# One five-block raw tile for each weight pair in place of two tiles, the sums written over blocks already split, three such tiles

## The chip, the core and the metric

The kernel runs on one core of a Trainium2 chip. The core has a matrix engine (TensorE, PE in the rows), VectorE (DVE), ScalarE (ACT), GpSimd (POOL) and SyncE (SP, which here only starts DMA transfers), each with an instruction queue of its own that it works off in order. The metric is the device time of one execution in microseconds; the median of several runs is compared.

## The reference

The reference computes one layer of a decoder trunk on 512 tokens of width 1024, in float32:

```
h = rmsnorm(x, norm_g)
proj = h @ w_in               # 14 groups of columns, about 14,400 in all
yA = mLSTM(aq, ak, av, ai, af) * norm * sigmoid(ao) * silu(az)   # 4 heads of 256
yB = forgetting_attention(bq, bk, bv, bf) * silu(bz)             # 8 heads of 128
yC = multiscale_pool(cu) * silu(cz)                              # 4 groups of 256
merged = sum over n of sigmoid(gates[n]) * (y[n] @ w_branch[n])
out = rmsnorm(x + merged @ w_out, final_g)
```

The kernel is free in how it multiplies, as long as the float32 result is met.

## The kernel before

**Split products.** Each float32 matrix is split into a high part (`hi`, a cast to a rounded format on ScalarE, `hi_of`, line 288) and a low part (`lo`, the difference, on VectorE, `lo_of`, line 291). A product is then three matmuls (`mm3`, lines 300 to 302): hi by hi, hi by lo, lo by hi.

**Units and pairs.** The weights are read in the order that `plan()` gives. A unit ("U") is one weight tile of 128x1024 that is loaded, split and multiplied as it is. A pair ("P") is two column groups of 128 that are multiplied together by a seven-product scheme of the Strassen kind: the 1024x256 weight block is seen as four blocks of 128x512 (Q = 512 columns in memory), and the products need sums of them. There are 42 pairs. For each, the kernel before keeps two raw tiles: R, 128x1536, with the three blocks b2_1, b1_0, b1_1 as loaded, and T, 128x2048, whose first two blocks are loaded as b2_1 and b1_0. GpSimd then starts a DMA that adds the block b2_0 onto both (line 377), and VectorE adds two further blocks (T2 = T1 + R0 and T3 = T2 + R2, lines 392 and 396). The splits are called parts: j = 0 takes the last two blocks of R, j = 1 the first of R, j = 2 takes T1 and T2, j = 3 takes T0 and T3. PE uses them in the order 0, 0, 2, 2, 3, 1, 3, twelve matmuls each, into the PSUM tiles `x`, `yz` and `y4` (function `pair`).

**Where raw data lies.** R and T have two buffers each. A unit takes a buffer of either kind, whichever is free first. The halves of a split go to one of four slots, and small tiles lie in a pool `w` of 11 buffers.

**What sets the order.** The instruction order is written by a planner at build time (`Flow`): it keeps a clock for each engine, gives each operation an estimated cost (`v_cost`, `a_cost`) and each transfer an estimated landing time (for the DMA that adds, 4.2 us after it is started), and records an operation on its engine when its estimated start has come. Nothing is reordered on the chip: an operation that waits holds up all that is recorded behind it on its engine. A transfer is started on SP when its buffer is free, in recorded order as well. The weight item numbers in tile names count the plan: `T16` is the second tile of item 16 (the pair ak_2, ak_3), `lo15_3` the low half of part 3 of item 15 (aq_2, aq_3), `raw43` the raw tile of unit 43 (a pool weight, "pw").

**Stages.** First head (units, to about 78 us), three mLSTM heads, pooling, four attention stages (pairs of bq and bk, units of bv, pairs of bz), the last gates (to about 689 us), then the branch products `wb` and the output product, which use units alone.

Of the kernel before, what the change touches and what calls it, by code (L numbers as in the profile page):

```python
# [7 lines left out]
F32 = mybir.dt.float32  # L8
# [5 lines left out]
P = 128  # L14
S = 512
D = 1024
KT = D // P
NT = S // P
AH = 4
# [10 lines left out]
SWITCH = 1.3  # L30
NEAR = 4
PLAIN = 2

C_NG = 0
C_MNG = 8
# [53 lines left out]
def v_cost(n):  # L89
    return 0.15 + 1.05e-3 * n  # L90
# [16 lines left out]
class Flow:  # L107
# [39 lines left out]
    def settle(self, c):  # L147

        while c.alive:
            kind = c.req[0]  # L150
            if kind == "get":
                t = self.grab(*c.req[1:])
                if t is None:
                    return False
                self.resume(c, t)
            elif kind == "any":
                names = [n for n in c.req[1] if self.free[n]]
                if not names:
                    return False
                n = min(names, key=lambda n: self.free[n][0])  # L160
                self.resume(c, (n, self.grab(n)))
# [88 lines left out]
def trunk(tc, x, xt_in, w, wpair, cols, fg, out):  # L250
    nc = tc.nc
    with contextlib.ExitStack() as ctx:
# [14 lines left out]
                index.append(np_)  # L267
                np_ += 1

        for name, n in (("R", 2), ("T", 2), ("slot", SLOTS), ("s3", 1), ("C", 5), ("E", 2), ("w", 9),  # L270
                        ("qk", 2), ("v", 1), ("pm", 1), ("em", 1), ("mx", 4), ("pj", 4), ("S", 8),
                        ("f", 2), ("nf", 1)):
            fl.stock(name, n)
# [2 lines left out]
            return st.tile(list(shape), dt, tag="b", name=name, bufs=28)  # L276

        def work(name, shape=(P, S), dt=F32):
            return st.tile(list(shape), dt, tag="w", name=name, bufs=11)

        def mx(name):
            return ps.tile([P, S], F32, tag="mx", name=name, bufs=4)
# [27 lines left out]
        fed = [4]  # L310
        used = [0]

        def raw_tile(tag, name, n):
            return st.tile([P, n], F32, tag=tag, name=name, bufs=2)

        at_use, n_ = [], 0
        for it in order:
# [8 lines left out]
        def feed_unit(i):  # L326
            what = order[i][1:]
            n = width(what)
            own = what[0] == "pw"
            prio = late(i, 0)  # L330

            def gen():
                if not own:
                    ts = yield ("get", "slot", 1)
                tag, t = yield ("any", ("R", "T"))
                t = yield ("SP", 0.06, t)
                raw = raw_tile(tag, f"raw{i}", n)
# [12 lines left out]
                lo_of(lo, raw, hi)  # L350
                fl.put(tag, 1, t)
                chunks[i, 0] = (hi, lo)
                fl.done["c", i, 0] = t
            fl.add(gen(), prio)

        def feed_pair(i):
            tiles = {}
            src = wpair[index[i]]
            left = {"R": 4, "T": 2}

            def drop(tag, t):
                left[tag] -= 1
                if not left[tag]:
                    fl.put(tag, 1, t)
# [17 lines left out]
            def parts(j, n, name, raw, tag):  # L382
                def gen():
                    ts = yield ("get", "s3" if j == 1 else "slot", 1)
                    t = yield ("wait", (tag, i))
                    if j >= 2:
                        if j == 3:
                            t = yield ("wait", ("sum", i))
                        r, s_ = tiles["R"], tiles["T"]
                        t = yield ("DVE", v_cost(Q), t)  # L390
                        if j == 2:
                            add(s_[:, 2 * Q:3 * Q], s_[:, Q:2 * Q], r[:, :Q])
                            fl.done["sum", i] = t
                            drop("R", t)
                        else:
                            add(s_[:, 3 * Q:], s_[:, 2 * Q:3 * Q], r[:, 2 * Q:])
                            drop("R", t)
                    t = yield ("ACT", a_cost(n), max(t, ts))
                    shape = (P, n) if j < 3 else (P, 2, Q)
                    mk = work if j == 1 else b  # L400
                    hi, lo = [mk(f"{x_}{i}_{j}", shape, F32R) for x_ in ("hi", "lo")]
                    hi_of(hi, raw())
                    t = yield ("DVE", v_cost(n), t)
                    lo_of(lo, raw(), hi)
                    drop("R" if j < 2 else "T", t)
# [5 lines left out]
            parts(0, 2 * Q, "s0", lambda: tiles["R"][:, Q:], "R")  # L411
            parts(2, 2 * Q, "a", lambda: tiles["T"][:, Q:3 * Q], "T")
            parts(1, Q, "s3", lambda: tiles["R"][:, :Q], "R")
            parts(3, 2 * Q, "b", lambda: tiles["T"].rearrange("p (a c) -> p a c", a=4)[:, 0::3], "T")

        def feed(n):
            while fed[0] < min(n, len(order)):
# [30 lines left out]
        def pair(a, c, into, after):  # L448
# [8 lines left out]
            def prod(o, j, half, mov, start, stop, last=False):  # L457
                fl.need(("c", i, j))
                ws = chunks[i, j]
                ws = [(t_[:, half] if j == 3 else t_[:, half * Q:(half + 1) * Q])  # L460
                      .rearrange("p (k c) -> p k c", c=P) for t_ in ws]
# [25 lines left out]
            prod(x_[:, :H], 2, 1, sig["s2"], False, True, last=True)  # L487
            side(x_[:, :H], e[:, 1], -1.0)
            y4 = bank("y4")
            prod(y4[:, :H], 3, 1, sig["A22"], True, True)  # L490
# [14 lines left out]
            prod(x_[:, :H], 3, 0, sig["s3"], False, True, last=True)  # L505
# [22 lines left out]
            nc.sync.dma_start(out=xt, in_=x[t * P:(t + 1) * P, :])  # L528
            xs.append(xt)

        raws = [raw_tile("RRTT"[i], f"raw{i}", D) for i in range(4)]

        def fill(i, part, parts):
            n = D // parts
# [62 lines left out]
                first_split(1, k * HEAD // KT, HEAD)  # L597
        fill(2, 0, 1)
        x_load(0)
        fill(3, 0, 1)  # L600
        x_load(1)
        first_split(2, 0, 1)
        x_square(0)
# [7 lines left out]
            r_diag(t)  # L611
        hi_of(dgh, dg)
        lo_of(dgl, dg, dgh)
        for name in ("slot", "R", "T"):
            fl.free[name] = []
        fl.grab("w", 3)
        fl.t.update(ACT=14.0, DVE=14.0)
# [442 lines left out]
        def first_head():  # L1060
# [11 lines left out]
                fl.t["PE"] += 1.4  # L1072
                fl.pos += 1
            fl.put("R", 2, 0.0)
            fl.put("T", 2, 8.0)
            fl.put("slot", 2)
            feed(8)
            fl.tick()
# [622 lines left out]
def pack(np, w_in, pool_w, w_branch, w_out):  # L1701
# [74 lines left out]
```

## Time and profile before

| what | value |
| --- | --- |
| median of 3 runs | 889.76 us (887.24 to 890.56) |
| the profiled execution | 891.74 us, its span 889.8 us |
| PE busy | 854.9 us, 96% |
| VectorE, ScalarE, GpSimd busy | 625.3, 507.9, 100.8 us |
| mean granted TensorE clock | 0.987 of full |

The span runs from the first to the last instruction; the profiled execution's own time is 1.94 us longer. Busy time of PE is modelled and holds stretches at a lower clock, so the rows of a stretch say more than the share over the span. A row of a timeline gives in brackets how long the engine stood idle before the instruction, and who ended that.

### The profile page before, as it was taken

How to read it: one execution, taken by the hardware profiler on the slowest of the kernel's cores; microseconds unless marked ns; L12 is line 12 of the kernel's file. 1: busy time of each engine (PE TensorE's matmuls, PEld its weight loads, DVE VectorE, ACT ScalarE, POOL GpSimd, SP SyncE). 2: the span in 40 equal slices, each digit the busy share in tenths (PEclk: the TensorE clock that was granted, in tenths of full speed). 3: DMA queues.
4: the chain of work that ended last, by engine and by line, in shares of the span. 5: the costliest groups of instructions: out<-in, count | busy, mean ns of one | idle time of the engine just before them, and what ended most of it. 6: DMA issues, size and time to landing. Idle time of an engine off the chain costs nothing.

```text
span 889.8 us, 14985 instructions
## 1 busy us (share of the span) xinstructions
PE 854.9 (96%) x5954; PEld 801.6 (90%) x5954; DVE 625.3 (70%) x985; ACT 507.9 (57%) x865; POOL 100.8 (11%) x135
## 2 busy tenths in 40 slices
PE   9999799999999999789899999999998999999997
PEld 7888799999999999689899999999988978888886
DVE  4889799587789668698877686686686763445623
ACT  7569589778687566354556565564565653102313
POOL 0002211111102010011211111211211000000020
PEclk9999899999999999989999999999998999999999
DMA  9326566746655556566556547447556786464302
GB/s 347 108 71 187 141 171 178 190 119 178 186 153 144 171 152 200 135 166 189 168 118 202 157 128 195 131 132 207 149 151 181 264 301 227 163 238 139 96 23 95
DMA packets 48998, 147.95 MB, mean 166 GB/s; under 512 B 4884, under 2 KB 5268, under 8 KB 48928
## 3 DMA queue, kind: packets, MB, share of 16 engines
q1 hardware_dynamic: 36000, 121.19, 38.4%
q0 software_dynamic: 12208, 24.67, 17.4%
q8 instruction: 47, 0.77, 0.4%
q10 hardware_dynamic: 720, 1.13, 0.4%
q14 instruction: 23, 0.19, 0.1%
HBM read 132.26 MB, written 14.70 MB: 165 GB/s over the span
## 4 chain that ended last, share of the span: by engine, by line
PE 59%; DMA 19%; DVE 13%; ACT 4%; issue 4%; SPq 0%; DVEq 0%; POOLq 0%; ACTq 0%
DMA T<-w_pairs 11%; DVE lo L291 6%; PE wb L302 5%; PE wb L301 5%; PE wb L300 5%; DMA raw<-w_units 4%; DMA nfb<-rows 3%; ACT hi L288 3%; PE av L301 2%; PE av L302 2%; PE out L302 2%; PE out L300 2%; PE av L300 2%; PE out L301 2%; DVE T L294 1%
## 5 line engine op out<-in xcount | busy, mean ns | idle before, releaser
L288 ACT CAST hi<-T 128x1024 fp32r<-128x1024 f32 x84 | 88.0, 1048 | 63.9 <-DVE T L294 59.0
L291 DVE TENSOR_TENSOR lo<-T,hi 128x1024 fp32r<-128x1024 f32 x84 | 102.6, 1224 | 15.1 <-ACT hi L288 14.6
L288 ACT CAST hi<-raw 128x1024 fp32r<-128x1024 f32 (+3 forms) x65 | 64.9, 1011 | 84.2 <-DMA raw<-w_units 41.3
L291 DVE TENSOR_TENSOR lo<-raw,hi 128x1024 fp32r<-128x1024 f32 (+3 forms) x65 | 75.7, 1174 | 38.1 <-ACT hi L288 38.0
L377 POOL DMA_DIRECT2D T<-w_pairs x42 | 51.1, 1216 | 436.7 <-DMA T<-w_pairs 187.5
L294 DVE TENSOR_TENSOR T<-T,R 128x512 f32<-128x512 f32 x84 | 58.6, 697 | 39.1 <-DMA T<-w_pairs 34.7
L291 DVE TENSOR_TENSOR lo<-R,hi 128x1024 fp32r<-128x1024 f32 x84 | 80.0, 954 | 5.8 <-ACT hi L288 5.4
L288 ACT CAST hi<-R 128x1024 fp32r<-128x1024 f32 x84 | 69.2, 836 | 0.5 <-DMA R<-w_pairs 0.4
L1601 DVE TENSOR_TENSOR gt<-wb,gt 128x512 f32<-128x512 f32 x16 | 11.1, 692 | 37.3 <-PE wb L302 37.3
L300 PE MATMUL bv<-hi,hT 128*128 128x256 f32 x128 | 36.6, 286 | 0.0
L302 PE MATMUL bv<-hi,hT 128*128 128x256 f32 x128 | 36.2, 282 | 0.0
L301 PE MATMUL bv<-lo,hT 128*128 128x256 f32 x128 | 36.1, 282 | 0.0
L1404 POOL TENSOR_SCALAR_AFFINE_SELECT s<-s 128x128 f32<-128x128 f32 x32 | 20.9, 686 | 81.3 <-DVE s L1400 81.1
L300 PE MATMUL av<-hi,hT 128*128 128x256 f32 x96 | 27.2, 284 | 0.0
L301 PE MATMUL av<-lo,hT 128*128 128x256 f32 x96 | 27.2, 283 | 0.0
L302 PE MATMUL av<-hi,hT 128*128 128x256 f32 x96 | 27.2, 283 | 0.0
L1421 ACT ACTIVATE s<-s,mx 128x128 f32<-128x128 f32 (+3 forms) x32 | 17.9, 563 | 15.7 <-DVE mx L1413 15.7
L288 ACT CAST m<-mg 128x512 fp32r<-128x512 f32 x8 | 5.0, 621 | 38.3 <-DVE mg L294 38.3
L301 PE MATMUL out<-lo,m 128*128 128x512 f32 (+1 forms) x72 | 26.3, 365 | 0.0
L302 PE MATMUL out<-hi,m 128*128 128x512 f32 (+1 forms) x72 | 26.3, 365 | 0.0
L300 PE MATMUL out<-hi,m 128*128 128x512 f32 (+1 forms) x72 | 26.3, 365 | 0.0
L302 PE MATMUL wb<-yc,lo 128*128 128x512 f32 x64 | 24.9, 389 | 0.0
(2187 smaller groups left out, 3338.9 us busy)
## 6 DMA issues: line engine op xcount, KB each, us to landing
R<-w_pairs SPq DMA_DIRECT2D x42, 768.0 KB, 4.5
raw<-w_units SPq DMA_DIRECT2D x58, 512.0 KB, 4.3
T<-w_pairs SPq DMA_DIRECT2D x42, 512.0 KB, 5.1
T<-w_pairs POOLq DMA_DIRECT2D x42, 512.0 KB, 6.6
g<-g SPq DMA_DIRECT2D x12, 512.0 KB, 4.5
yf<-y SPq DMA_DIRECT2D x24, 256.0 KB, 5.5
gt<-g SPq DMA_DIRECT2D x24, 256.0 KB, 4.3
xT<-x_turned SPq DMA_DIRECT2D x8, 256.0 KB, 5.4
```

Source lines behind the costliest of these rows:

```text
L288: nc.scalar.copy(out=hi, in_=full)
L291: nc.vector.tensor_tensor(out=lo, in0=full, in1=hi.bitcast(F32), op=ALU.subtract)
L294: nc.vector.tensor_tensor(out=out_, in0=a, in1=c, op=ALU.add)
L300: nc.tensor.matmul(out_, lhsT=ah, rhs=bh, start=start, stop=False, **kw)
L301: nc.tensor.matmul(out_, lhsT=ah, rhs=bl, start=False, stop=False, **kw)
L302: nc.tensor.matmul(out_, lhsT=al, rhs=bh, start=False, stop=stop, **kw)
L377: nc.gpsimd.dma_start(out=s_[:, :2 * Q].rearrange("p (a c) -> p a c", a=2), in_=src[:, 3 * Q:].unsqueeze(1).to_broadcast([P, 2, Q]), accum ...
L1404: nc.gpsimd.affine_select(out=ss[i][:, q0:n], in_=ss[i][:, q0:n], pattern=[[-1, P]], compare_op=ALU.is_ge, fill=NEG, base=0, channel_multi ...
L1421: nc.scalar.activation(out=s_, in_=s_, func=AF.Exp, bias=ms[i][0], accum_out=sme)
L1601: nc.vector.tensor_tensor(out=g_, in0=o, in1=g_, op=ALU.mult)
```

## The change

A pair has one tile R of 128x2560, five blocks, with three buffers that units share. The blocks in memory are reordered to b1_0, b1_1, b2_1, b2_0. Blocks 3 and 4 are loaded first, as b1_0 and b2_1 (two pieces of 2 KB in each row in place of one of 4 KB), then blocks 0 to 2 by a second transfer right behind it on SP. GpSimd's DMA adds b2_0 onto blocks 3 and 4 as before. The two sums of VectorE are written over blocks 0 and 1, whose split (j = 0) was made before. The two halves of parts 2 and 3 change places, and the products ask for them so. The buffer comes free when all four parts are split. The planner's landing estimates are raised (for the adding DMA from 4.2 to 6.2 us, for a load of a unit from 3.4 to 4.2), the pool `w` has 10 buffers in place of 11, and the fourth raw tile of the first stage waits for a buffer of the first.

```diff
+RAWS = 3
-        for name, n in (("R", 2), ("T", 2), ("slot", SLOTS), ("s3", 1), ("C", 5), ("E", 2), ("w", 9),
+        for name, n in (("R", RAWS), ("slot", SLOTS), ("s3", 1), ("C", 5), ("E", 2), ("w", 8),
...
-                tag, t = yield ("any", ("R", "T"))
+                t = yield ("get", "R", 1)
...
+                    yield ("wait", ("av", AH - 1))
                     ts = yield ("get", "v", 1)
-                t = max(t + 3.4, ts)
+                t = max(t + 4.2, ts)
...
-                r = tiles["R"] = raw_tile("R", f"R{i}", 3 * Q)
-                nc.sync.dma_start(out=r, in_=src[:, :3 * Q])
-                fl.done["R", i] = t + 4.2
-                t = yield ("get", "T", 1)
+                r = raw_tile(f"R{i}", 5 * Q)
+                nc.sync.dma_start(out=r[:, 3 * Q:].rearrange("p (a c) -> p a c", a=2),
+                                  in_=src.rearrange("p (a c) -> p a c", c=Q)[:, 0:3:2])
+                t1 = t + 4.5
                 t = yield ("SP", 0.06, t)
-                s_ = tiles["T"] = raw_tile("T", f"T{i}", 4 * Q)
-                nc.sync.dma_start(out=s_[:, :2 * Q], in_=src[:, :2 * Q])
-                t = yield ("POOL", 0.9, t + 3.4)
-                nc.gpsimd.dma_start(out=s_[:, :2 * Q].rearrange("p (a c) -> p a c", a=2),
+                nc.sync.dma_start(out=r[:, :3 * Q], in_=src[:, :3 * Q])
+                fl.done["R", i] = t + 5.0
+                t = yield ("POOL", 0.9, t1)
+                nc.gpsimd.dma_start(out=r[:, 3 * Q:].rearrange("p (a c) -> p a c", a=2),
                                     in_=src[:, 3 * Q:].unsqueeze(1).to_broadcast([P, 2, Q]),
                                     accum_op=ALU.add)
-                fl.done["T", i] = t + 4.2
+                fl.done["T", i] = t + 6.2
...
                         if j == 2:
-                            add(s_[:, 2 * Q:3 * Q], s_[:, Q:2 * Q], r[:, :Q])
+                            add(r[:, :Q], r[:, 3 * Q:4 * Q], r[:, 2 * Q:3 * Q])
...
-                            add(s_[:, 3 * Q:], s_[:, 2 * Q:3 * Q], r[:, 2 * Q:])
+                            add(r[:, Q:2 * Q], r[:, :Q], r[:, Q:2 * Q])
...
-            prod(yz[:, H:], 2, 0, sig["s1"], True, True)
+            prod(yz[:, H:], 2, 1, sig["s1"], True, True)
...
-            pairs.append(np.concatenate([b2[:, 1], b1[:, 0], b1[:, 1], b2[:, 0]], axis=1))
+            pairs.append(np.concatenate([b1[:, 0], b1[:, 1], b2[:, 1], b2[:, 0]], axis=1))
```

The order of instructions moves at many places. Two of them follow. On VectorE, at the end of the first pair (item 15), before:

```order
L294 TENSOR_TENSOR T16_797<-T16_797,R16_750 128x512
L752 SCALAR_TENSOR_TENSOR gr_z_628<-gr_r_630,gr_u_629 72x512
L291 TENSOR_TENSOR lo15_3_906<-T15_722,hi15_3_905 128x1024
L755 TENSOR_SCALAR gr_u_629<-gr_z_628 8x512
L291 TENSOR_TENSOR lo16_0_923<-R16_750,hi16_0_922 128x1024
```

and now:

```order
L286 TENSOR_TENSOR lo16_0_870<-R16_763,hi16_0_869 128x1024
L286 TENSOR_TENSOR lo15_3_923<-R15_720,hi15_3_922 128x1024
L768 SCALAR_TENSOR_TENSOR gr_r_630<-gr_z_628 4x512
L286 TENSOR_TENSOR aql0_791<-cvaq01_717,aqh0_790 128x512
L772 TENSOR_SCALAR gr_z_628<-gr_r_630 4x512
L286 TENSOR_TENSOR akl0_826<-cvak01_767,akh0_825 128x512
L777 TENSOR_TENSOR gr_u_629<-gr_u_629,gr_r_630 4x512
L997 SCALAR_TENSOR_TENSOR gA0_356<-ao0_590,cs_71,gA0_356 128x512
L289 TENSOR_TENSOR aq1_988<-aq_2_aq_3yz_894,aq_2_aq_3e_892 128x2x256
L289 TENSOR_TENSOR R16_763<-R16_763 128x512
```

The first sum of item 16, which needs the adding DMA of that item, stood ahead of the last split of item 15 and now stands eight instructions behind it. On SP, in the pooling stage (items 40 to 47; `y03` and `y20` are stores of results), before:

```order
L370 DMA R41_3969<-w_pairs 128x1536
L338 DMA raw43_3980<-w_units 128x1024
L987 DMA y03_207<-gA3_3170 128x1024
L1221 DMA y20_212<-cz0_3898 128x1024
L375 DMA T41_4081<-w_pairs 128x1024
L370 DMA R42_4101<-w_pairs 128x1536
L370 DMA R44_4261<-w_pairs 128x1536
L375 DMA T42_4285<-w_pairs 128x1024
L1221 DMA y21_213<-cz1_4188 128x1024
L375 DMA T44_4350<-w_pairs 128x1024
```

and now:

```order
L368 DMA R41_3786<-w_pairs 128x2x512
L372 DMA R41_3786<-w_pairs 128x1536
L368 DMA R42_3934<-w_pairs 128x2x512
L372 DMA R42_3934<-w_pairs 128x1536
L333 DMA raw43_4062<-w_units 128x1024
L989 DMA y03_207<-gA3_3155 128x1024
L1223 DMA y20_212<-cz0_3881 128x1024
L368 DMA R44_4226<-w_pairs 128x2x512
L372 DMA R44_4226<-w_pairs 128x1536
```

All of pair 42 is loaded ahead of the unit 43 and of two stores now; its second tile T42 stood seven transfers later.

## Rows read from the trace of the kernel before

**Rows 1.** Page, part 1: busy time of each engine, share of the span, instructions.

```profile
PE 854.9 (96%) x5954; PEld 801.6 (90%) x5954; DVE 625.3 (70%) x985; ACT 507.9 (57%) x865; POOL 100.8 (11%) x135
```

**Rows 2.** PE's waits, 22 to 884 us: waiter, whom for, us in total, times, longest.

```profile
PE cz_cz_5yz L300 <- ACT hi L288: 5.2, 1, 5.2
PE aq_aq_3y L302 <- DVE lo L291: 4.9, 1, 4.9
PE g_g_3y L302 <- DVE lo L291: 4.0, 1, 4.0
PE py L300 <- DVE s L1400: 2.5, 1, 2.5
PE bq_bk_5yz L300 <- ACT bq_bk_5e L473: 1.7, 1, 1.7
...
PE cu_cu_5yz L302 <- DVE lo L291: 1.5, 1, 1.5
PE g_g_1y L302 <- DVE lo L291: 1.2, 1, 1.2
PE cu_cu_5yz L300 <- ACT hi L288: 1.0, 1, 1.0
...
```

**Rows 3.** Stretches: us, busy (instructions) by engine, granted clock, DMA share, GB/s.

```profile
98.00:102.00 4.00, 4.00 (x23) 4.00 (x23) 3.41 (x4) 2.99 (x7) 1.11 (x2) 0.57 0.44 138
358.00:363.00 5.00, 2.54 (x20) 2.13 (x19) 4.76 (x9) 3.19 (x5) 0.00 (x0) 1.00 0.00 0
...
382.00:386.00 4.00, 4.00 (x25) 4.00 (x25) 3.00 (x5) 0.93 (x2) 0.00 (x0) 0.66 1.03 305
...
680.00:688.00 8.00, 8.00 (x46) 7.87 (x45) 3.73 (x5) 1.31 (x4) 1.20 (x1) 0.68 0.70 215
689.00:845.00 156.00, 156.00 (x760) 131.22 (x759) 87.26 (x113) 54.98 (x72) 2.70 (x5) 1.00 0.59 204
104.00:108.00 4.00, 4.00 (x36) 4.00 (x35) 3.83 (x8) 1.99 (x4) 3.45 (x3) 1.00 0.65 83
...
```

**Rows 4.** VectorE's timeline, 88 to 98 us: start, duration, instruction, idle before.

```profile
94.54 0.69 DVE L294 TENSOR_TENSOR T<-T,R 128x512 f32<-128x512 f32 x1 [5.56 <-DMA T<-w_pairs]
...
96.28 1.20 DVE L291 TENSOR_TENSOR lo<-T,hi 128x1024 fp32r<-128x1024 f32 x1
```

**Rows 5.** Line 377, GpSimd's adding DMA, whole run: who waits, time to landing.

```profile
DVE T L294: 34.7, 11
...
DMA to landing us min/median/max: 6.3/6.6/10.3
```

**Rows 6.** SP's timeline, 336 to 385 us: start, duration of the issue, instruction.

```profile
338.41 0.33 SPq L338 DMA_DIRECT2D raw<-w_units  x1
...
365.02 0.33 SPq L375 DMA_DIRECT2D T<-w_pairs  x1
...
371.29 0.33 SPq L375 DMA_DIRECT2D T<-w_pairs  x1
```

**Rows 7.** GpSimd's timeline, 344 to 390 us.

```profile
370.39 1.21 POOL L377 DMA_DIRECT2D T<-w_pairs  x1 [18.51 <-DVE cz L1335]
```

**Rows 8.** VectorE's timeline, 369 to 380 us.

```profile
370.04 1.22 DVE L291 TENSOR_TENSOR lo<-raw,hi 128x1024 fp32r<-128x1024 f32 x1
...
378.27 0.69 DVE L294 TENSOR_TENSOR T<-T,R 128x512 f32<-128x512 f32 x1 [3.95 <-issue]
```

**Rows 9.** Page, part 6: DMA issues, count, KB each, median us to landing.

```profile
R<-w_pairs SPq DMA_DIRECT2D x42, 768.0 KB, 4.5
raw<-w_units SPq DMA_DIRECT2D x58, 512.0 KB, 4.3
T<-w_pairs SPq DMA_DIRECT2D x42, 512.0 KB, 5.1
```

**Rows 10.** Page, part 5: the splits and sums of pairs, busy and mean ns.

```profile
L291 DVE TENSOR_TENSOR lo<-T,hi 128x1024 fp32r<-128x1024 f32 x84 | 102.6, 1224 | 15.1 <-ACT hi L288 14.6
...
L294 DVE TENSOR_TENSOR T<-T,R 128x512 f32<-128x512 f32 x84 | 58.6, 697 | 39.1 <-DMA T<-w_pairs 34.7
```

More of the change, by code (lines that the diff above doesn't have):

```diff
@@ L155, in settle @@
                 self.resume(c, t)
[L156 to L161, printed above, removed]
             elif kind == "wait":
@@ L278, in work @@
         def work(name, shape=(P, S), dt=F32):
-            return st.tile(list(shape), dt, tag="w", name=name, bufs=11)
+            return st.tile(list(shape), dt, tag="w", name=name, bufs=10)
         def mx(name):
@@ L311, in trunk, with raw_tile @@
         used = [0]
-        def raw_tile(tag, name, n):
-            return st.tile([P, n], F32, tag=tag, name=name, bufs=2)
+        def raw_tile(name, n):
+            return st.tile([P, n], F32, tag="R", name=name, bufs=RAWS)
         at_use, n_ = [], 0
@@ L356, in feed_pair, with blocks @@
         def feed_pair(i):
-            tiles = {}
+            cell = []
             src = wpair[index[i]]
[L359 to L364, printed above, removed]
+            left = [4]
+            def blocks(j):
+                return cell[0].rearrange("p (a c) -> p a c", c=Q)[:, (slice(0, 2), slice(2, 3),
+                                                                     slice(0, 4, 3), slice(1, 5, 3))[j]]
             def load():
@@ L378, in load, with parts @@
+                nc.gpsimd.dma_start(out=r[:, 3 * Q:].rearrange("p (a c) -> p a c", a=2),
                                     in_=src[:, 3 * Q:].unsqueeze(1).to_broadcast([P, 2, Q]),
                                     accum_op=ALU.add)
-                fl.done["T", i] = t + 4.2
-            def parts(j, n, name, raw, tag):
+                fl.done["T", i] = t + 6.2
+            def parts(j, n, key):
                 def gen():
                     ts = yield ("get", "s3" if j == 1 else "slot", 1)
-                    t = yield ("wait", (tag, i))
+                    t = yield ("wait", (key, i))
@@ L386, in gen @@
                     if j >= 2:
[L387 to L390, printed above, removed]
+                        t0 = yield ("wait", ("s0" if j == 2 else "sum", i))
+                        r = cell[0]
+                        t = yield ("DVE", v_cost(Q), max(t, t0))
                         if j == 2:
-                            add(s_[:, 2 * Q:3 * Q], s_[:, Q:2 * Q], r[:, :Q])
+                            add(r[:, :Q], r[:, 3 * Q:4 * Q], r[:, 2 * Q:3 * Q])
@@ L393, in gen @@
                             fl.done["sum", i] = t
-                            drop("R", t)
                         else:
-                            add(s_[:, 3 * Q:], s_[:, 2 * Q:3 * Q], r[:, 2 * Q:])
-                            drop("R", t)
+                            add(r[:, Q:2 * Q], r[:, :Q], r[:, Q:2 * Q])
                     t = yield ("ACT", a_cost(n), max(t, ts))
-                    shape = (P, n) if j < 3 else (P, 2, Q)
+                    shape = (P, n // Q, Q)
                     mk = work if j == 1 else b
@@ L401, in gen @@
                     hi, lo = [mk(f"{x_}{i}_{j}", shape, F32R) for x_ in ("hi", "lo")]
-                    hi_of(hi, raw())
+                    hi_of(hi, blocks(j))
                     t = yield ("DVE", v_cost(n), t)
-                    lo_of(lo, raw(), hi)
-                    drop("R" if j < 2 else "T", t)
+                    lo_of(lo, blocks(j), hi)
+                    if j == 0:
+                        fl.done["s0", i] = t
+                    left[0] -= 1
+                    if not left[0]:
+                        fl.put("R", 1, t)
@@ L410, in feed_pair @@
             fl.add(load(), 0)
[L411 to L414, printed above, removed]
+            parts(0, 2 * Q, "R")
+            parts(2, 2 * Q, "T")
+            parts(1, Q, "R")
+            parts(3, 2 * Q, "T")
         def feed(n):
@@ L459, in prod @@
                 ws = chunks[i, j]
-                ws = [(t_[:, half] if j == 3 else t_[:, half * Q:(half + 1) * Q])
-                      .rearrange("p (k c) -> p k c", c=P) for t_ in ws]
+                ws = [t_[:, half].rearrange("p (k c) -> p k c", c=P) for t_ in ws]
                 for k in range(4):
@@ L484, in pair @@
             prod(yz[:, :H], 0, 1, sig["A12"], True, True, last=True)
-            prod(yz[:, H:], 2, 0, sig["s1"], True, True)
+            prod(yz[:, H:], 2, 1, sig["s1"], True, True)
             side(yz[:, H:], e[:, 2])
-            prod(x_[:, :H], 2, 1, sig["s2"], False, True, last=True)
+            prod(x_[:, :H], 2, 0, sig["s2"], False, True, last=True)
             side(x_[:, :H], e[:, 1], -1.0)
             y4 = bank("y4")
-            prod(y4[:, :H], 3, 1, sig["A22"], True, True)
+            prod(y4[:, :H], 3, 0, sig["A22"], True, True)
             t4 = side(y4[:, :H], e[:, 3])
@@ L504, in pair @@
             fl.put("pj", 1, t)
-            prod(x_[:, :H], 3, 0, sig["s3"], False, True, last=True)
+            prod(x_[:, :H], 3, 1, sig["s3"], False, True, last=True)
             t = fl.now("DVE", v_cost(H))
@@ L529, in x_load, with fill_last @@
             xs.append(xt)
-        raws = [raw_tile("RRTT"[i], f"raw{i}", D) for i in range(4)]
+        raws = [raw_tile(f"raw{i}", D) for i in range(RAWS)]
+        def fill_last():
+            raws.append(raw_tile("raw3", D))
+            fill(3, 0, 1)
         def fill(i, part, parts):
@@ L599, in trunk @@
         x_load(0)
-        fill(3, 0, 1)
+        fill_last()
         x_load(1)
@@ L613, in trunk @@
         lo_of(dgl, dg, dgh)
-        for name in ("slot", "R", "T"):
+        for name in ("slot", "R"):
             fl.free[name] = []
@@ L1074, in first_head @@
             fl.put("R", 2, 0.0)
-            fl.put("T", 2, 8.0)
+            fl.put("R", 1, 12.0)
             fl.put("slot", 2)
```

5 lines of the change are left out of this document (3 added, 2 removed).

## The prediction

> **What bounds the kernel now.** I read the page first: PE is busy 854.9 of 889.8 us, VectorE 70%, ScalarE 57% [rows 1]. So the change can give back only what PE loses: 34.9 us of idle time, some of it at the two ends, and the time that it ran at a lower clock. The waits of PE say where. Six of them belong to pairs whose last parts were not split in time [rows 2]: 5.2 (`cz_cz_5yz`, item 42), 4.9 (`aq_aq_3y`, item 15), 4.0 (`g_g_3y`, item 71), 1.5 and 1.0 (`cu_cu_5yz`, item 41) and 1.2 (`g_g_1y`, item 70), together 17.8 us. Two, 2.5 and 1.7, follow late loads of units (bv). Seven more of 0.8 and less, and some of the two ends, make up the rest.
>
> The table of stretches then shows what each of the three long waits left behind it: PE came back at the lower of its two levels (1.2 in place of 2.4 GHz) for some us. A mean granted clock of 0.57 over 4 us, 0.66 over 4 us and 0.68 over 8 us, with PE busy all the time, costs 4 x 0.43 + 4 x 0.34 + 8 x 0.32 = 5.6 us [rows 3].
>
> Why the parts were late: in the timeline of VectorE, the sum T of item 16 stood idle 5.56 us for the adding DMA of its own pair; only then, at 96.28, came the split that PE was waiting for, the last of item 15 [rows 4]. It stood behind the sum in the queue and needed nothing of it. VectorE waited so for the adding DMA 11 times, 34.7 us in all; that DMA lands 6.3 to 10.3 us after its issue, in the middle 6.6 [rows 5], where the planner had reckoned with 4.2 us after a start of 0.9. The second long wait is of another kind: T42 could be loaded only at 365.02 [rows 6], its adding DMA started when that load had landed, at 370.39 [rows 7], and its first sum at 378.27 [rows 8]. One of the two T buffers was held all this time by the raw tile of unit 43, loaded at 338.41 [rows 6] and split at 370.04 [rows 8] (its target tile is the one in which the values of another stage lie); the next T load went out right behind that split, at 371.29 [rows 6].
>
> **What the change takes away.** No operation falls away: still two loads and one adding DMA for each of 42 pairs, two sums, four splits. What changes is when they can start. In the order, the sum of item 16 now stands behind the last split of item 15, and both loads of item 42 stand ahead of unit 43. I counted in the built program how many matmuls are recorded between a pair's adding DMA and its first sum: before 21 to 201, in the middle 91, and for 13 of the 42 fewer than 63; now 50 (item 15, where they are the wide ones of 512 columns) and else 100 to 291, in the middle 196. In a full stretch 36 matmuls take 4.00 us [rows 3], 0.111 each. So the middle lead goes from about 10 to about 22 us, and the shortest but the first from 2.3 to 11.1, more than the longest landing, 10.3 [rows 5]. The first has 50 wide matmuls, each about twice as long, about 11 us again. I therefore take all six waits as gone: 17.8 us, and with the three long ones the lower clock, 5.6 us.
>
> That holds if the loads start early enough. In the pooling stage T42 waited for a T buffer until 365.02 [rows 6]. Now item 42 needs the buffer of item 39, whose splits were over before unit 43 was loaded into another of them at 338.41 [rows 6]: some 26 us earlier, for a wait of 5.2.
>
> **What it costs, in bounds.** *The first load* moves rows of 2 KB in place of 4 KB, and the second one queues behind it. Nearest rows: the T load, 5.1 us, behind an R load on the same queue as a rule, and the adding DMA, which also moves 2 KB pieces, 6.6 [rows 5, 9]. So 0 to 1.5 us later, and blocks 0 to 2 the same, against 4.5 for R alone [rows 9]. I take 1; it is covered by the 11 us and more, and without that cover each late pair would stop VectorE's queue for as long. *Sums and splits* keep their sizes: the split of T0 and T3 already ran with a step of three blocks in the 1224 ns group, the sum in the 697 ns one [rows 10]; a sum in place has no row of its own, and I take it between no change and one more such sum, 0 to 0.7 us, on an engine with 30% of its time free [rows 1], and nearer to no change, since it reads and writes as much as before. *Units* have three raw buffers in place of four. In the branch products PE is busy for the whole of 156.00 us [rows 3]; a load lands in 4.3 us [rows 9], and the program keeps some 90 wide matmuls between a load and its cast there before, about 40 now: some 9 us. So nothing; without that cover it would be up to 4.3 for each of the units. *One buffer fewer in `w`* delays only stores and reloads that this stretch hides as well. *New tight places*: part 2 of items 16, 18 and 25 is now split only 5 to 8 matmuls ahead of its use, under 0.9 us. Below nothing is lost there, above one split each, 1.22 us [rows 10], and its half of a wait: 0 to 4 us. I take 2, since the planner had such places before too (items 24 and 41 with 7) and one of those two waited.
>
> *What a wider supply can't do.* While PE waited at 358 to 363 us, the DMA engines moved nothing, share 0.00 [rows 3]; bandwidth was not short there, a free buffer was. The Trainium skill, "DMA: Bandwidth & Descriptors", section "Issuing engines are not separate DMA queues", says that transfers started by any engine run on the same 16 DMA engines and interleave. By that a third pair in flight brings no byte sooner and makes the adding DMA of the pair in need slower; the sum by it would give back part of the 23 us, as in the first rival below. At 382 to 386 us the share was 1.03 [rows 3], so in bursts the trace agrees.
>
> **The sum.** The profiled execution took 891.74 us, its span 889.8. 891.74 - 17.8 - 5.6 + 2 = 870.3. It lies 2.0 above the median of the runs, so 868.3, rounded to 868. The two waits on units, 4.2 us, and the small ones I leave as they are.
>
> **Rivals.** *The transfers collide.* Three pairs may be in flight, and loads go out in twos, so adding DMAs take their longest, 10.3, and loads theirs, some 8: 18.6 us from the first load. The program leaves about 15 matmuls between load and adding DMA, so 153 would be wanted behind that; 11 of 42 pairs have fewer, on average 122, and each would stop VectorE for 3.4 us, 38 us together. Before, 34.7 us of such stops cost PE 17.8 [rows 2, 5]; so up to 20 us come back. Half of that, with the loads late only now and then, gives 878; for it speaks the full share in bursts, against it the mean share of 0.59 to 0.66 in full stretches [rows 3].
>
> *The wait moves into VectorE's own work.* While PE waited at 358 to 363, VectorE was busy 4.76 of 5.00 us [rows 3]. If the splits themselves are the limit wherever pooling or attention work is dense, the long waits come back as waits for splits: 885 to 893, no change. Against it: before that stretch VectorE stood and waited for the DMA, and the work had piled up.
>
> *Slower: too few raw tiles beside units.* A unit that waits for its slot or its target holds one of three tiles, as unit 43 did for 33 us [rows 6, 8]. Two units (each av and bv stage has two) leave one for pairs. A pair holds its tile for 5.1 + 6.6 us and some 5 to 8 us of sums and splits [rows 5, 9, 10], about 18. PE takes 84 x 0.111 = 9.3 us for a pair and 96 x 0.111 = 10.7 for the two units, 20 together, so one tile just suffices. It would cost time once a pair holds its tile over 20 us; to make the kernel 0.5% slower the seven such stages must lose (17.8 + 5.6 + 4.4) / 7 = 4.0 us each, so a hold of 24 us: 894 to 905. Before, R and T had four buffers, and units could leave a pair one of each as well.
>
> **How the numbers follow.** Forecast, 857 to 873 us: 0.64. Transfers collide, 873 to 885: 0.18. The wait moves: 0.10. Slower: 0.08. The low end is the sum with the two waits on units gone too and 5 of what else PE idled: 891.74 - 22.0 - 5.6 - 5 - 2.0 = 857. Up to 884 the range takes in the collisions: 857 to 884. Within 0.5%, 885.3 to 894.2, is about what a measurement of this kernel can't tell from no change. Faster by more than that: 0.64 + 0.18 = 0.82; the same 0.10; slower 0.08.
>
> **What the profile after would show.** VectorE's waits for the adding DMA fall from 34.7 to under 10 us; PE's waits at `aq_aq_3y`, `cz_cz_5yz`, `cu_cu_5yz`, `g_g_1y` and `g_g_3y` are gone, and the granted clock is full from the first head to the tail. If the adding DMA lands in over 9 us as a rule, the collisions are right. If PE waits as long but for splits while VectorE is busy throughout, the wait has moved. If SP stands before pair loads for longer behind units, in the av and bv stages, tiles are too few. Wrong at the root I would be if PE's idle time came mostly from something other than the pairs' supply.

## The result: 865.08 us, 2.6% faster

| | before | after |
| --- | --- | --- |
| median | 888.50 us (885.16 to 890.56, 4 runs) | 865.08 us (863.41 to 866.42, 4 runs) |
| the profiled execution | 891.74 us, span 889.8 | 866.04 us, span 864.0 |
| PE busy | 854.9 us | 846.2 us |
| mean granted clock | 0.987 | 0.996 |

The ratio is 0.974, 95% interval 0.970 to 0.978. The forecast was 868, its range 857 to 884.

First part 1 of the page after, as in [rows 1]:

```profile
span 864.0 us, 14971 instructions
PE 846.2 (98%) x5954; PEld 796.1 (92%) x5954; DVE 626.6 (73%) x985; ACT 509.9 (59%) x865; POOL 96.2 (11%) x135
```

The number of matmuls is the same, and VectorE and ScalarE work as long as before [rows 1]. PE's idle time fell from 34.9 to 864.0 - 846.2 = 17.8 us, and its busy time by 8.7: together 25.8, the difference of the spans up to rounding.

Then all waits of PE after, those of the first 22 us left out, as in [rows 2]:

```profile
PE tpB L1445 <- DVE s L1402: 2.3, 1, 2.3
PE ak_ak_3yz L295 <- ACT ak_ak_3e L471: 1.8, 1, 1.8
PE aq_aq_7x L295 <- ACT aq_aq_7e L471: 1.7, 1, 1.7
PE aq_aq_3y L297 <- DVE lo L286: 1.4, 1, 1.4
PE av L296 <- DVE lo L286: 1.1, 1, 1.1
...
PE ak_ak_3yz L297 <- DVE lo L286: 0.8, 1, 0.8
...
PE ao_ao_5yz L297 <- DVE lo L286: 0.6, 1, 0.6
PE py L295 <- DVE s L1402: 0.4, 1, 0.4
```

Of the six waits of pairs in [rows 2], one is left, `aq_aq_3y`, 1.4 in place of 4.9. The two on units went as well: `py` from 2.5 to 0.4, `bq_bk_5yz` from 1.7 to nothing. New near the top are two waits for a side copy of ScalarE (line 471), 1.8 and 1.7; `tpB`, now the first, had 1.6 us in three places before. All rows of this view add up to 27.4 us before and 10.1 after; with those of the first 22 us it is 28.9 and 12.1.

The cause as the prediction saw it shows in the view of line 375, the adding DMA (line 377 before, [rows 5]):

```profile
DVE R L289: 1.5, 1
...
DMA to landing us min/median/max: 6.4/6.9/11.2
```

VectorE waited for it once, 1.5 us, in place of 11 times and 34.7 us; the DMA itself got no faster. What grew is the distance. Measured in the trace from the start of the adding DMA's issue to the start of the pair's first sum (which of them belong together is read from the program), it is 10.3 us in the middle before, with 12 of the 42 under 8 us, and 22.6 after, with 10.2 the shortest. The stretches of [rows 3], and the one place where the clock was still low, 108 to 116 us:

```profile
108.00:116.00 8.00, 6.54 (x34) 6.07 (x35) 4.54 (x8) 6.75 (x14) 1.94 (x2) 0.79 0.69 162
...
98.00:102.00 4.00, 4.00 (x38) 3.87 (x36) 4.00 (x8) 3.37 (x6) 1.29 (x1) 1.00 0.51 186
358.00:363.00 5.00, 5.00 (x44) 5.00 (x44) 5.00 (x9) 2.49 (x4) 0.00 (x0) 1.00 0.41 127
```

Between 98 and 102 the clock is full now (0.57 before), and between 358 and 363 PE is busy all the time (2.54 of 5.00 before).

### The profile page after: what moved, and what is told of

Its sections match the earlier page's. It is cut to its first block, busy times and chain, and to the rows that moved or that the text cites. A ratio compares the mean times of both kernels' runs of the same rounds, so it can differ in the third digit from the quotient of the medians.

```text
span 864.0 us, 14971 instructions
## 1 busy us (share of the span) xinstructions
PE 846.2 (98%) x5954; PEld 796.1 (92%) x5954; DVE 626.6 (73%) x985; ACT 509.9 (59%) x865; POOL 96.2 (11%) x135
## 3 DMA queue, kind: packets, MB, share of 16 engines
q0 software_dynamic: 12208, 24.67, 17.5%
## 4 chain that ended last, share of the span: by engine, by line
PE 80%; DMA 7%; DVE 5%; ACT 5%; issue 1%; SPq 0%; POOL 0%; DVEq 0%; ACTq 0%; POOLq 0%
PE wb L296 5%; PE wb L295 5%; PE wb L297 5%; DMA nmb<-rows 3%; DVE lo L286 2%; PE out L295 2%; PE out L296 2%; PE out L297 2%; DMA R<-w_pairs 2%; PE bv L296 1%; PE bv L297 1%; PE bv L295 1%; PE av L296 1%; PE av L297 1%; ACT hi L283 1%; PE av L295 1%
## 5 line engine op out<-in xcount | busy, mean ns | idle before, releaser
L286 DVE TENSOR_TENSOR lo<-R,hi 128x1024 fp32r<-128x1024 f32 (+1 forms) x168 | 180.4, 1085 | 41.4 <-ACT hi L283 40.8
L283 ACT CAST hi<-R 128x1024 fp32r<-128x1024 f32 (+1 forms) x168 | 155.1, 945 | 33.8 <-DVE R L289 24.4
L283 ACT CAST hi<-raw 128x1024 fp32r<-128x1024 f32 (+3 forms) x65 | 65.3, 1012 | 84.0 <-DMA raw<-w_units 62.5
L375 POOL DMA_DIRECT2D R<-w_pairs x42 | 51.1, 1216 | 382.7 <-DMA R<-w_pairs 173.1
L289 DVE TENSOR_TENSOR R<-R 128x512 f32<-128x512 f32 x84 | 58.0, 690 | 2.3 <-DMA R<-w_pairs 1.5
L296 PE MATMUL wb<-yc,hi 128*128 128x512 f32 x64 | 24.9, 389 | 0.0
L295 PE MATMUL wb<-yc,hi 128*128 128x512 f32 x64 | 24.9, 389 | 0.0
L295 PEld LDWEIGHTS bv<-hi,hT 128*128 128x128 f32 x128 | 24.5, 191 | 0.2
L296 PEld LDWEIGHTS bv<-lo,hT 128*128 128x128 f32 x128 | 24.5, 191 | 0.2
```

Source lines behind the costliest of these rows:

```text
L283: nc.scalar.copy(out=hi, in_=full)
L286: nc.vector.tensor_tensor(out=lo, in0=full, in1=hi.bitcast(F32), op=ALU.subtract)
L289: nc.vector.tensor_tensor(out=out_, in0=a, in1=c, op=ALU.add)
L295: nc.tensor.matmul(out_, lhsT=ah, rhs=bh, start=start, stop=False, **kw)
L296: nc.tensor.matmul(out_, lhsT=ah, rhs=bl, start=False, stop=False, **kw)
L375: nc.gpsimd.dma_start(out=r[:, 3 * Q:].rearrange("p (a c) -> p a c", a=2), in_=src[:, 3 * Q:].unsqueeze(1).to_broadcast([P, 2, Q]), accum_ ...
```

## Experiments

The theory: TensorE waited because VectorE's queue was held by the adding DMA's landing, and the change puts more work between that DMA and the first sum. Rivals: the planner's raised estimates do it alone; the third tile is what matters; the order of the two loads is. "Before" and "after" are the two kernels; the ratio is always to runs of the kernel before on the same chip (887.1 to 887.3 us). The kernel after was not timed again beside them. So where a row is compared with after, the ratios are the fairer measure (after has 0.974, 0.970 to 0.978), and a difference of times in us is uncertain by some 3 us.

| kernel | us, median (lowest to highest) | ratio, 95% interval |
| --- | --- | --- |
| e1, before without the adding DMA | 859.33 (858.68 to 860.03) | 0.970 (0.966 to 0.973) |
| e2, after, old estimates | 866.68 (865.88 to 867.50) | 0.978 (0.975 to 0.981) |
| e3, before, raised estimates | 878.13 (876.94 to 879.00) | 0.991 (0.988 to 0.994) |
| e4, after, two tiles | 887.97 (885.64 to 891.38) | 1.002 (0.999 to 1.004) |
| e5, before, T loaded first | 865.18 (863.19 to 866.31) | 0.977 (0.974 to 0.979) |
| e6, after, blocks 0 to 2 first | 860.09 (858.55 to 861.53) | 0.971 (0.969 to 0.973) |
| e7, after without the adding DMA | 858.48 (857.66 to 859.72) | 0.969 (0.967 to 0.972) |
| e8, after, rows reckoned later | 857.88 (857.50 to 860.04) | 0.969 (0.967 to 0.971) |
| e9, e6 and e8 together | 856.73 (855.85 to 857.24) | 0.965 (0.961 to 0.969) |
| e10, plan of e6, loads as after | 862.26 (860.73 to 864.91) | 0.972 (0.968 to 0.976) |
| e11, e5 with all estimates raised | 868.90 (866.08 to 875.01) | 0.980 (0.975 to 0.984) |
| e12, before, one `w` buffer less | 893.43 (887.90 to 896.39) | 1.006 (1.002 to 1.009) |

### Is it the wait for the adding DMA? (e1, e7)

```diff
-                nc.gpsimd.dma_start(out=s_[:, :2 * Q].rearrange("p (a c) -> p a c", a=2),
-                                    in_=src[:, 3 * Q:].unsqueeze(1).to_broadcast([P, 2, Q]),
-                                    accum_op=ALU.add)
```

> The kernel before with the DMA that adds block 3 left out: its 42 issues on GpSimd are gone, so blocks 3 and 4 of the sums lack that addend and the outputs are other numbers; every other instruction stands where it stood. Theory (VectorE's queue, held by this DMA's landing, is what TensorE waited for): the six waits of pairs, 17.8 us, and most of the 5.6 us of lower clock go, 866 to 872 us; VectorE waits for no pair's DMA longer than some 5 us in all. Rival (the loads themselves come late, since two pairs of tiles let too few of them fly): T tiles are loaded at the same places as before, so most of the waits stay, 880 us or more.

859.33 us. With the tiles and places of before, and only this DMA gone, PE's list of waits begins at 1.2 us:

```profile
PE cz_cz_5yz L300 <- ACT hi L288: 1.2, 1, 1.2
PE warm_ps L551 <- POOL ones L544: 1.0, 1, 1.0
PE g_g_5x L300 <- ACT g_g_5e L470: 0.9, 1, 0.9
```

VectorE's list has no wait for a pair's DMA at all. So the loads were early enough, and the rival (loads too late) falls. The gain, 28 us, is larger than the 23.4 that the prediction put on the six waits and the clock; a kernel without this DMA also moves 22 MB less and its waits on units go too (`py` 0.6), so what of the other 5 us is the queue and what the transfers is not told apart here (e5 keeps the DMA and moves it; the part on the prediction comes back to the units).

The same edit in the kernel after:

> The kernel after with the DMA that adds block 3 left out (42 issues on GpSimd; blocks 3 and 4 lack that addend, the outputs are other numbers), all else where it stood. Theory (after, this DMA is waited for by 1.5 us alone, but its traffic slows the small loads of gate rows, whose landing took 5.9 to 10.8 us and which held TensorE for 5 to 6 us): 858 to 862 us, with nmb and nfb landing in 3 to 6 us. Rival (the waits left are the splits', whatever the transfers do): 863 to 866 us.

858.48 us, inside what the theory gave. Before, this DMA cost 28 us; after, 4 by the ratios and 6.6 by the medians. The landing of `nmb` fell from 5.9/6.1/10.8 to 3.1/5.8/6.7 us (least, middle, most), that of `nfb` from 3.3/5.4/8.6 to 3.2/3.9/7.1. PE's list of waits begins with 1.8 us at `ak_ak_3yz`, as after; `tpB`, `aq_aq_7x` and `aq_aq_3y` are gone. What the small loads cost with this DMA in place, e8 shows.

### The planner's numbers (e2, e3)

```diff
-                t = max(t + 4.2, ts)
+                t = max(t + 3.4, ts)
...
-                t1 = t + 4.5
+                t1 = t + 3.4
...
-                fl.done["R", i] = t + 5.0
+                fl.done["R", i] = t + 4.2
...
-                fl.done["T", i] = t + 6.2
+                fl.done["T", i] = t + 4.2
```

> The kernel after with the planner's landing times put back to those of before (3.4 us for a unit and for the load that the adding DMA follows, 4.2 us for blocks 0 to 2 and for the adding DMA). In the program the counts of matmuls between the adding DMA and the first sum are the same as after (median 196, 50 the least). Theory (three tiles, so that a pair is loaded earlier): no change, 865 us, 862 to 868. Rival (the raised estimates made the planner put the sums later): back towards before, 875 to 889 us.

866.68: once there are three tiles the raised estimates are worth little, if anything (the intervals of e2 and after overlap).

> The kernel before, with its two pairs of tiles, and only the landing times in the planner raised to those that the trace of before shows (5.0 us for the load ahead of the adding DMA, 6.2 us for that DMA, 4.5 us for blocks 0 to 2, 4.2 us for a unit). In the program 5 of 42 pairs have under 63 matmuls (7 us) between the adding DMA and the first sum, in place of 13. Theory (tiles, and the order that they allow): part of the gain, some 880 us, 874 to 886. Rival (estimates alone): all of it, 865 to 869 us.

878.13, as the theory had it: about 9 of the 23 us. VectorE still waits 17.5 us, 7 times, for the adding DMA.

### Third tile or order of the loads? (e4, e5, e11)

e4 sets `RAWS = 2`, and the four loads at the start take the two tiles in turn.

> The kernel after with two five-block tiles in place of three (the four loads at the start take two and two). In the program the adding DMA stands a median of 101 matmuls ahead of the first sum, 196 with three tiles, 4 of 42 pairs under 63; units' splits end 1 or 2 matmuls behind the place where they are needed in three items. Theory (the third tile is what the change brings): most of the gain is lost and units wait as well, 882 us, 874 to 895. Rival (five blocks in one tile and the order of the loads bring it): 865 to 870 us.

887.97: not most of the gain is lost, but all of it. PE's list begins with 4.8 and three waits of 3.2 us, and VectorE's wait for the adding DMA is back:

```profile
DVE R L289 <- DMA R<-w_pairs: 24.0, 9, 5.2
```

Two five-block tiles are fewer buffers than R and T, two of each, since a unit takes a whole one; so e4 shows that this layout needs three, not that two pairs in flight are too few. That is what e5 asks (its edit; the T load is moved ahead of the R load):

```diff
+                t = yield ("get", "T", 1)
+                t = yield ("SP", 0.06, t)
+                s_ = tiles["T"] = raw_tile("T", f"T{i}", 4 * Q)
+                nc.sync.dma_start(out=s_[:, :2 * Q], in_=src[:, :2 * Q])
+                t1 = t + 3.4
                 t = yield ("get", "R", 1)
...
-                t = yield ("get", "T", 1)
-                t = yield ("SP", 0.06, t)
-                s_ = tiles["T"] = raw_tile("T", f"T{i}", 4 * Q)
-                nc.sync.dma_start(out=s_[:, :2 * Q], in_=src[:, :2 * Q])
-                t = yield ("POOL", 0.9, t + 3.4)
+                t = yield ("POOL", 0.9, t1)
```

> The kernel before, with its two pairs of tiles and its estimates, and only the two loads of a pair exchanged: the T tile (blocks 0 and 1, what the adding DMA waits for) is asked for and loaded first, the R tile second. In the program the adding DMA stands a median of 125 matmuls ahead of the first sum (91 before, 196 after), 3 of 42 pairs under 63. Theory (what counts is how far the adding DMA lies ahead of the first sum, by whatever means): over half of the gain, 872 us, 868 to 878, with VectorE's wait for this DMA under 15 us. Rival (only a third pair in flight brings it): 880 to 888 us, as T tiles are still held by units.

865.18, the time of the kernel after, with the old tiles, the old estimates and no new layout. VectorE's waits for pairs' DMAs in it:

```profile
DVE T L294 <- DMA R<-w_pairs: 8.4, 3, 5.1
DVE T L294 <- DMA T<-w_pairs: 1.3, 2, 0.9
```

The wait for the adding DMA is 1.3 us. So the theory holds in its general form (how far the DMA lies ahead of the sum), and the claim that it takes a third tile falls. What counts is the distance as it runs, not as it is recorded. In the program e4 (101 matmuls in the middle, 4 pairs under 63) comes near e5 (125, 3 under 63), but there the loads wait longer for buffers: in the traces the first sum starts 11.5 us in the middle behind the adding DMA's issue in e4, with 6 of 42 under 8 us, and 14.4 in e5, with one.

The first of PE's waits in e5 are these:

```profile
PE cz_cz_3yz L300 <- ACT cz_cz_3e L474: 2.6, 1, 2.6
PE py L300 <- DVE s L1401: 1.9, 1, 1.9
PE cz_cz_5x L300 <- ACT cz_cz_5e L474: 1.8, 1, 1.8
```

Two of them lie in pooling, where R, now the second load, comes late. There the third tile has its own worth; PE from 300 to 400 us, first e5 and then after:

```profile
300.00:400.00 100.00, 95.61 (x751) 93.36 (x750) 77.14 (x121) 54.06 (x95) 10.44 (x16) 0.98 0.62 166
```

```profile
300.00:400.00 100.00, 100.00 (x810) 98.66 (x810) 80.89 (x126) 57.29 (x100) 10.93 (x17) 1.00 0.69 191
```

After loses elsewhere what it gains here, at 84 to 132 us, near 244 and near 439, where small row loads are waited for (next part). With these out of the way the two layouts should differ:

> The kernel before with its two pairs of tiles, the T load first, and all landing times in the planner raised (4.5, 5.0 and 6.2 us for a pair, 4.2 for a unit, 9.0 and 8.0 for the row loads). Theory (three tiles give nothing that a better order with two pairs doesn't give, but for the leads, 123 matmuls in the median and 12 or more on a first split where three tiles have 23): 860 us, 857 to 866. Rival (with the rows' waits out of the way the third tile is worth some 5 us or more): 863 to 870 us against 856 to 858 with three tiles.

868.90, against 856.73 for three tiles on the same chip (e9): the rival holds. In e11 PE's three longest waits are `cu_cu_5yz` 3.5, `cz_cz_3yz` 2.1 and `cz_cz_5yz` 1.9, all in pooling, where unit 43 held a buffer from 326.26 to its split at 370.89, as before [rows 6, 8]. The higher estimates did not help this layout either, 0.980 against 0.977 in e5. That this buffer is the cause is read from the trace; the wait that the change sets ahead of such a unit's target was not tried alone.

### The waits that after has new (e6, e8, e9, e10)

In ScalarE's timeline of the kernel after the side copy that PE waits for at `aq_aq_7x` is recorded behind exponentials that need `nmb`, a row of gates spread by a small DMA:

```profile
242.12 1.28 ACT L826 ACT_TABLE_LOAD   x1 [3.23 <-DMA nmb<-rows]
243.41 0.61 ACT L826 ACTIVATE e<-nmb,aT 128x384 f32<-128x384 f32 x1
243.94 0.35 ACT L471 COPY aq_aq_7e<-aq_aq_7x 128x256 f32<-128x256 f32 x1
```

SP had issued that DMA at 231.25, right behind the two loads of a pair, and it landed after 10.8 us; the planner reckons 2.5. At `ak_ak_3yz` it is the same (5.9 us, and then a mask that GpSimd makes of it), and at `tpB` it is VectorE and `nfb` (7.9 us). e8 raises these two estimates alone:

```diff
-            t = yield ("POOL", 0.9, t + 2.5)
+            t = yield ("POOL", 0.9, t + 9.0)
...
-                tn += 2.5
+                tn += 8.0
```

> The kernel after, in which the planner reckons 9.0 us in place of 2.5 for the landing of a row of gates (nmb, ahead of the exponentials) and 8.0 in place of 2.5 for that of nfb, so that ScalarE's exponentials and VectorE's scores stand later in their queues, behind the side copies and splits that TensorE needs. Theory (these small loads, behind pair loads that now come in threes, hold ScalarE and VectorE): the waits of ak_ak_3yz, aq_aq_7x and tpB go, some 5 us, 860 us, 857 to 864. Rival (the same places turn into waits of the scores themselves): 865 to 870 us.

857.88; against after that is 7 us by the medians and 4 by the ratios, whose intervals just touch (0.967 to 0.971, and 0.970 to 0.978). At this place ScalarE still waits for `nmb`, 3.72 us, but now the copy stands ahead of the waiting instruction:

```profile
234.65 0.37 ACT L471 COPY aq_aq_7e<-aq_aq_7x 128x256 f32<-128x256 f32 x1 [0.55 <-PE aq_aq_7x L297]
...
239.25 1.28 ACT L826 ACT_TABLE_LOAD   x1 [3.72 <-DMA nmb<-rows]
```

The landing of `nmb` was even longer, 5.7/6.8/12.3 us, so it was the order and not the transfer that cost time; the waits of `ak_ak_3yz` for its copy, `aq_aq_7x` and `tpB` are gone.

> The kernel after with the two loads of a pair exchanged: blocks 0 to 2 first, the load that the adding DMA waits for second. The first sum comes 176 matmuls (median) behind the adding DMA in the program, 196 after; 40 the least, item 15, 50 after. Theory (with three tiles the distance is long enough in either order): 866 us, 863 to 870, the wait of aq_aq_3y about 1 us longer. Rival (the order of the loads is what the change brings): 872 us or more.

860.09, where I expected 1 us worse than after: by the medians it is 5 us better, by the ratios under 3, with intervals that overlap (0.969 to 0.973, and 0.970 to 0.978). In the program TensorE and VectorE have the order of after; that on ScalarE differs in 10 places and that on GpSimd in 27, though the estimates differ by 0.56 us only: the copy of `aq_aq_7` stands ahead of the exponential here too. e10 takes these queues and exchanges only the two issues on SP again:

> The kernel with the order of instructions on TensorE, VectorE, ScalarE and GpSimd that blocks 0 to 2 first had (860.1 us), word for word, and the two loads of a pair issued on SyncE as after (the load for the adding DMA first). Theory (the 5 us between after and that kernel come from the order that the planner's other landing times gave: the side copy of aq_aq_7 stands ahead of the exponential that waits for nmb): 860 us, 857 to 863. Rival (they come from the transfers, long rows first): 865 us, 863 to 867.

862.26 lies in the theory's range and just under the rival's, its runs (860.73 to 864.91) in both, and its interval overlaps those of e6 and after; the time alone does not decide. Its waits divide the two causes: `aq_aq_7x` is gone as in e6, so that is the order; `aq_aq_3y` (1.4) and `tpB` (1.9) are there as after and not in e6, so these hang on which load goes first. (VectorE's wait for the adding DMA is 1.4 us here, 1.5 after and 0.7 in e6; e6 has a new wait of 1.4 at `ak_ak_5yz` instead.) How much each is worth in time, the runs don't separate beyond that.

> The kernel after with blocks 0 to 2 loaded first and the row loads reckoned at 9.0 and 8.0 us: the two edits that each ran faster than after by themselves (860.1 and 857.9 us). Theory (both took away the same waits behind small row loads, so they don't add): 856 us, 853 to 859. Rival (they are separate gains, 5 and 7 us): 853 us or less.

856.73, as the theory that they overlap had it, and clear of the kernel after (the intervals of the ratios are 0.961 to 0.969 and 0.970 to 0.978). This is the fastest version found, though its interval overlaps that of e8; its list of PE's waits begins:

```profile
PE av L296 <- DVE lo L286: 1.3, 1, 1.3
PE warm_ps L556 <- POOL ones L549: 1.0, 1, 1.0
PE ak_ak_3yz L297 <- DVE lo L286: 0.8, 1, 0.8
```

### One buffer less in `w` (e12)

```diff
-("C", 5), ("E", 2), ("w", 9),
+("C", 5), ("E", 2), ("w", 8),
...
-            return st.tile(list(shape), dt, tag="w", name=name, bufs=11)
+            return st.tile(list(shape), dt, tag="w", name=name, bufs=10)
```

> The kernel before with one work buffer less (10 in place of 11, 8 in place of 9 in the planner's stock), the part of the change that the prediction priced at nothing. In the program 17 of 42 pairs have under 63 matmuls between the adding DMA and the first sum, 13 before. Theory by the count of short distances: 892 us, 887 to 897. Rival (nothing, as predicted): 884 to 890 us.

893.43: 0.6% slower by itself, with VectorE's wait for the adding DMA up from 34.7 to 48.6 us in 15 places. The price of nothing was wrong for this part alone. That with three tiles the longer distances cover it is likely, but the kernel after with 11 buffers was not run.

## Why the prediction was right, point by point

**The cause** holds: the gain is the end of VectorE's waits for the adding DMA. e1 takes the DMA away and the gain is there; e5 keeps it, brings it earlier by another means, and the gain is there too.

**The six waits, 17.8 us**, were to go as a whole; 1.4 is left at `aq_aq_3y`. The prediction gave item 15 a lead of about 11 us over a longest landing of 10.3. The chain of waits after, at 73 to 85 us, shows that this DMA took longer:

```profile
73.26 11.24 DMA R<-w_pairs
```

**The clock, 5.6 us**: the three low stretches are gone, and there is a new one behind the new wait at `ak_ak_3yz`. The term was too small: the stretches that I took began after PE had come back. From where it came back, before and, in the last line, after:

```profile
97.50:102.00 4.50, 4.47 (x23) 4.47 (x24) 3.87 (x5) 3.48 (x8) 1.11 (x2) 0.56 0.39 123
380.20:385.50 5.30, 4.83 (x24) 4.54 (x25) 4.30 (x7) 1.48 (x3) 0.00 (x0) 0.57 0.93 224
679.40:686.00 6.60, 6.57 (x34) 6.57 (x35) 4.33 (x6) 1.47 (x4) 1.18 (x1) 0.57 0.68 240
...
109.40:114.00 4.60, 4.54 (x19) 4.07 (x20) 2.33 (x4) 4.60 (x12) 1.23 (x1) 0.63 0.61 98
```

That is 4.47 x 0.44 + 4.83 x 0.43 + 6.57 x 0.43 = 6.9 us before and 4.54 x 0.37 = 1.7 after. So 5.2 of the 8.7 us by which PE's busy time fell are the clock in these stretches; I can't assign the other 3.5.

**Waits on units, left in the sum as they were (4.2 us)**, is the term that was off: 0.4 is left. I had put them down to late loads of units, and the trace of before bears that out: at both places ScalarE waits for a unit's load.

```profile
431.50 1.05 ACT L288 CAST hi<-raw 128x1024 fp32r<-128x1024 f32 x1 [1.91 <-DMA raw<-w_units]
...
559.75 1.04 ACT L288 CAST hi<-raw 128x1024 fp32r<-128x1024 f32 x1 [4.26 <-DMA raw<-w_units]
```

Wrong was to take these loads as given. The two behind `py` landed in 6.2 and 6.8 us before. Without the adding DMA (e1) they took 3.5 and 4.2, and `py` waited 0.6. In e5 they took 6.6, and `py` waited 1.9, though VectorE stood only 1.3 us for the adding DMA. So VectorE's queue is not what held them; the landing goes with the wait, and in e1 it was shorter with fewer transfers about. After, the two landed in 3.4 and 3.5, issued 9 us apart. At `bq_bk_5yz` the units' loads still take 7.0 and 8.0 us after, but the copy that PE needs there is recorded ahead of the cast that waits longest.

**New tight places, taken at 2 us.** Part 2 of item 16 (`ak_ak_3yz`, 0.8) and another at `ao_ao_5yz` (0.6) did show, 1.4 us. Not in the sum were the new waits behind small row loads, 1.8 and 1.7 us and 0.7 more at `tpB`: 4.2 us. The working had looked only at the splits, not at what else stands in the queues once the splits are early.

**The sum.** Waits gone less new ones, 17.8 - 2 = 15.8, stand against 17.1 us less of idle time, and 5.6 us of clock against 8.7 less of busy time: 1.3 + 3.1 = 4.4 us more than forecast, the distance from 870.3 to the 866.04 of the profiled execution up to rounding. The 1.3 hides mistakes that nearly cancel, so that the idle time came out near the forecast is partly luck: the waits on units gave 3.8 more and other small ones 2.2 more, the new tight places cost 0.6 less, while the row loads cost 4.2 and `aq_aq_3y` kept 1.4; 0.3 is outside the rows of waits.

**The first load** was to land 0 to 1.5 us later, which it did not, and so were blocks 0 to 2, which they did. Part 6 of the page after, as in [rows 9]:

```profile
R<-w_pairs SPq DMA_DIRECT2D x42, 768.0 KB, 5.8
raw<-w_units SPq DMA_DIRECT2D x58, 512.0 KB, 3.8
R<-w_pairs SPq DMA_DIRECT2D x42, 512.0 KB, 4.5
R<-w_pairs POOLq DMA_DIRECT2D x42, 512.0 KB, 6.9
```

The load in pieces of 2 KB, now first, landed in 4.5 us against 5.1 for T; blocks 0 to 2, now second, in 5.8 against 4.5. In e5, whose T goes first in pieces of 4 KB, it is 4.0 and 5.5. So in the first place the pieces cost about 0.5 us, and the second place costs about 1 (in e6 0.7 for blocks 0 to 2 and 1.8 for the pieces).

**Units** with three raw buffers: no wait of PE in the branch products, as forecast. The count given for it was too high before: counted again in the program, the middle distance from load to cast is 67 matmuls before (not 90) and 43 after. ScalarE did wait longer for units' loads over the whole run, 62.5 us in place of 41.3 (part 5 of the pages, casts of `raw`), which cost PE nothing there.

**The sum in place** took no longer: 690 ns in the mean (page after, part 5) against 697 [rows 10].

**The buffer of item 42**: its first load goes out at 334.93 now, where T42 went out at 365.02 [rows 6], and PE is busy throughout that stretch. The held buffer was not the whole cause, though: in e1 unit 43 still holds one from 328.33 to 359.19, and the wait of 5.2 us at `cz_cz_5yz` is 1.2. That points to the late load and the adding DMA behind it together.

**The rivals.** The transfers did not collide as a rule: the adding DMA's middle landing rose from 6.6 to 6.9 us. (The rival was also priced too high: counted again in the program, 12 to 58 matmuls lie between the first load and the adding DMA, in the middle 27 and not 15.) The Trainium skill ("DMA: Bandwidth & Descriptors", section "Issuing engines are not separate DMA queues") has all transfers share the same 16 engines, whoever starts them; these 0.3 us agree with it, but are all that a third pair cost there. The wait did not move into VectorE's own work, which is 626.6 us as before. Too few tiles is what e4 shows with two; with three, no pair load came late enough to be seen in PE's waits.

## What to carry to other kernels

An engine that waits for a transfer holds everything recorded behind it, also work that needs nothing of that transfer; so give a planner the landing times that the trace shows (the longest for what stands in a shared queue), and put the urgent copies and splits ahead of the first instruction that waits. Before widening buffers, try to exchange two loads: start first the one with the longest chain behind it, here the load that a second DMA adds onto. That gave 22 us with two pairs of tiles (e5); with three tiles the distance suffices either way, and the other order (e6) was no slower. When one such wait is gone, read the list again: the next ones were small row loads that had been there all along, and two changed constants gave 4 to 7 us more (e8).

## What was not expected of the hardware

- A small transfer that spreads one row of gates over all partitions (256 KB) took 5.9, 6.1 and up to 10.8 us to land after, 12.3 in e8, as long as the adding DMA of 512 KB.
- The issue of a load on SP took 0.55 us where it went first in two pieces for each row (0.33 for the plain T or R load before), and 0.59 for the plain load right behind it; in e6, with the plain load first, 0.33 and 0.55.
- Taking 42 DMAs away made the kernel before 28 us faster and the kernel after 4 to 7, though each had landed in the same 6.6 to 6.9 us.
